# One step of a hybrid diffusion trunk: 32x32 blocks of the triangular inverses turned by TensorE products instead of VectorE transposes

## The chip, the cores and the metric

The kernel runs on one core of a Trainium2 chip. The time is device time of one launch in microseconds. The kernel before took 1106.6 us, the median of three runs (1103.13 to 1106.88). The changed kernel is timed in the same way.

## The reference, cut to what matters

One layer of a trunk works on 640 tokens: 128 context tokens and 512 latent tokens of width 1024. It normalises and modulates x, projects it with one matrix into the inputs of two mixers (a bidirectional RWKV-7 scan with 8 heads of 64, and grouped attention), joins their outputs in one projection, and ends with a gated ConvFFN of inner width 2816.

The change touches the RWKV scan alone. Per head, direction and token the reference does

```python
def step(s, inp):
    r_t, w_t, k_t, v_t, kk_t, a_t = inp
    sa = jnp.einsum('bhvk,bhk->bhv', s, -kk_t)
    s = (s * w_t[:, :, None, :]
         + sa[..., None] * (kk_t * a_t)[:, :, None, :]
         + v_t[..., None] * k_t[:, :, None, :])
    return s, jnp.einsum('bhvk,bhk->bhv', s, r_t)
```

The kernel does 64 tokens at a time. Inside such a chunk each token's correction depends on the earlier ones through a strictly triangular 64x64 matrix L, so that one chunk of one head needs the inverse of (1 - L). These inverses are what `inverse()` makes.

## The kernel before, in words

**Stages.** All of it is one program on five engines. By the profile's time line: the norm and the first projections (0 to about 130 us), the rest of the input projection beside the preparation of the scan (to about 218 us), the inverses, the first steps of the scan and the last projections (to about 310 us), attention beside the scan (to about 600 us), then output projection and FFN (to the end).

**The front.** `s_lora` (line 727) makes decay logits by products into PSUM banks of ring "mi" (two banks), `s_prep` (line 764) turns them on VectorE, ScalarE and GpSimd into AR and BK, and line 819 multiplies these into the matrices L, again into "mi"; line 823 masks them on VectorE into the SBUF tile LT: 128 partitions (two heads of 64 tokens), 32 matrices, 64 columns. Beside it `s_gemm` (line 499) runs the input projection on TensorE.

**The inverses.** There are three units, G0 (heads 0 to 3 of the latent tokens), CX (the context) and G1 (heads 4 to 7), and each calls `inverse` (line 829) once. A unit inverts the 32x32 diagonal blocks of its matrices by forward substitution, with one matrix entry per step for all blocks at once. For that it needs each block laid out along the free dimension of one partition. The kernel before does this with four VectorE transposes of 32x1024 (line 845, into tile Lt), then one addition of Lt and its own transposed view (line 854, into Ls), which folds both scan directions into one triangle. Ls then starts X (twelve small ScalarE copies, lines 858 to 864); 60 small operations follow (lines 870, 871), on VectorE for G0 and CX and on GpSimd for G1 (`EN_INV` is "VG", and G0 is given "V"). Two transposes of X (875, 877) give XT and XN; ScalarE copies their parts into MT (line 890, recorded at the helper's line 377); two sets of TensorE products, W (897, 898) and B (909, 910), fill the off-diagonal blocks, with Ws (901) between them and copies of B into MT behind them.

**Buffers.** G0 and CX share the tags i0 to i3 and the ring "inv" of size one: CX starts only when G0's B has been read out. G1 has tags of its own.

**What follows.** `s_chain` (1033) runs the scan: G0, then CX, then G1, each in two directions; line 1075 multiplies by MT. `s_gemm2` (line 539) makes the projections for g, q and k/v, line 570, in three PSUM banks of ring "tm"; each tile is copied to SBUF (`evac_tm`, line 528) and sent to DRAM (line 464). When gemm2 and G1's inverse are over, their SBUF pools are closed and attention starts by reading these tiles back (`s_norm`, line 1265).

**Order.** Each stage is a generator that yields its next piece of work with an engine and an assumed duration (`T` TensorE, `V` VectorE, `A` ScalarE, `G` GpSimd), or the wait for a ring or an event. `Flow.run` (line 313) keeps a time per engine and picks the piece that can start first, by priority among near ones. Each engine then executes its instructions strictly in the order so made. A wait `ring(name, 2)` is served when two of the ring's places are free.

Of the kernel before, what the change touches and what calls it, by code (L numbers as in the profile page):

```python
# [9 lines left out]
F32 = mybir.dt.float32  # L10
# [3 lines left out]
ALU = mybir.AluOpType  # L14
# [5 lines left out]
P = 128  # L20
# [27 lines left out]
def trunk(ctx: ExitStack, tc: tile.TileContext, a, o, dbg=None):  # L48
    nc = tc.nc
    te, ve, se, ge, sy = nc.tensor, nc.vector, nc.scalar, nc.gpsimd, nc.sync  # L50
# [6 lines left out]
    def nm(s):  # L57
        uid[0] += 1
        return f"{s}_{uid[0]}"
# [31 lines left out]
    mi = lambda s: psr.one("mi", s)  # L91
# [20 lines left out]
    ri = rip.__enter__()  # L112
# [4 lines left out]
    ident = cm2[:, 0:128]  # L117
# [115 lines left out]
    for b in range(4):  # L233
# [3 lines left out]
        g = st.tile([P, 512], F32, name=nm("g"), tag="g", bufs=2)  # L237
# [34 lines left out]
    class Flow:  # L272
# [12 lines left out]
        def ring(f, name, n):  # L285
            f.rings[name] = [f.now] * n
# [71 lines left out]
    def T(us):  # L358
        return ("w", (("T", us),), None, False)

    def V(n, par=False, k=1):
        return ("w", (("V", k * 0.065 + 1.07e-3 * n),), None, par)

    def A(n, tab=None, par=False, k=1):
        return ("w", (("A", k * 0.06 + 0.883e-3 * n),), tab, par)

    def G(us):
        return ("w", (("G", us),), None, False)
# [4 lines left out]
    def VA(n, par=False):  # L373
        return ("w", (("V", 0.065 + 1.07e-3 * n), ("A", 0.06 + 0.883e-3 * n)), None, par)

    def cpy(eng, dst, src):
        (se.copy if eng == "A" else ve.tensor_copy)(dst, src)  # L377
# [4 lines left out]
    def ev_(*key):  # L382
        return ("ev", key)

    flow = Flow()
# [27 lines left out]
    def s_wload(ph, jobs, pl, bufs):  # L413
        for i, dr in enumerate(units_of(jobs)):
            yield ring("raw")
            raw = pl.tile([P, 1024], F32, name=nm("raw"), tag="raw", bufs=bufs)
            sy.dma_start(raw, dr)
            wready["raw", ph, i] = raw
            yield Q(3.5)
            flow.done("raw", ph, i)  # L420
# [227 lines left out]
    G0, G1, CX = Group("g0", (0, 1), 2, 8), Group("g1", (2, 3), 2, 8), Group("ctx", (0, 1, 2, 3), 0, 2)  # L648
# [177 lines left out]
            flow.give(f"ab{d}")  # L826
            flow.done("ab", p, d)

    def inverse(g, en, pl, mp, sfx, rg, bank):
        eng = ve if en == "V" else ge  # L830

        def W(n, k=1):
            return V(n, k=k) if en == "V" else G(0.99 * (k * 0.1 + 2.2e-3 * n))

        nu, LT = g.nu, g.LT
        for p in g.pairs:
            for d in range(2):
                yield ev_("ab", p, d)
        yield ring("inv" + sfx)
        Lt = pl.tile([P, 1024], F32, name=nm("Lt"), tag="i0" + sfx)  # L840
        for qd in range(4):
            pr = slice(32 * qd, 32 * qd + 32)
            t0 = 32 * (qd % 2)
            yield V(1024)
            ve.transpose(Lt[pr].rearrange("p (t s) -> p t s", s=32), LT[pr, :, t0:t0 + 32].rearrange("p u t -> p t u"))
        Ls = pl.tile([P, 32, 32], F32, name=nm("Ls"), tag="i1" + sfx)
        X = pl.tile([P, 1024], F32, name=nm("X"), tag="i2" + sfx)
        X3 = X.rearrange("p (t s) -> p t s", s=32)
        Lt3 = Lt.rearrange("p (t s) -> p t s", s=32)
        yield G(1.0)  # L850
        ge.memset(X, 0.0)
        ge.memset(X[:, ::33], 1.0)
        yield W(1024)
        eng.tensor_tensor(Ls, Lt3, Lt3.rearrange("p t s -> p s t"), ALU.add)

        yield A(496, k=12)
        Lf = Ls.rearrange("p t s -> p (t s)")
        se.copy(X[:, 32::66], Lf[:, 32::66])
        for i in range(2):
            for j in range(2):  # L860
                se.copy(X[:, 64 + 32 * i + j::132], Lf[:, 64 + 32 * i + j::132])
        for b in (4, 8, 16):
            for q in range(0, 32, 2 * b):
                se.copy(X3[:, q + b:q + 2 * b, q:q + b], Ls[:, q + b:q + 2 * b, q:q + b])
        tmp = pl.tile([P, 256], F32, name=nm("tmp"), tag="i3" + sfx)
        for s in range(1, 31):
            n = 31 - s
            yield W(2 * n * s, k=2)
            t3 = tmp[:, :n * s].rearrange("p (t j) -> p t j", j=s)
            eng.tensor_tensor(t3, Ls[:, s + 1:32, s:s + 1].to_broadcast([P, n, s]), X3[:, s:s + 1, 0:s].to_broadcast([P, n, s]), ALU.mult)  # L870
            eng.tensor_tensor(X3[:, s + 1:32, 0:s], X3[:, s + 1:32, 0:s], t3, ALU.add)
        XT = pl.tile([P, 1024], F32, name=nm("XT"), tag="i0" + sfx)
        XN = pl.tile([P, 1024], F32, name=nm("XN"), tag="i1" + sfx)
        yield V(1024)
        ve.transpose(XT, X)
        yield V(1024)
        ve.transpose(XN.rearrange("p (j u) -> p j u", u=32), X3.rearrange("p i j -> p j i"))
        XT3 = XT.rearrange("p (i u) -> p u i", u=32)
        XN3 = XN.rearrange("p (j u) -> p u j", u=32)
        MT = mp[0].tile([P, 2 * nu, 64], F32, name=nm("MT"), tag=mp[1] or "MT" + g.nm)  # L880
        g.MT = MT
        yield G(2.0)
        ge.memset(MT, 0.0)
        fw, bw = slice(0, nu), slice(nu, 2 * nu)
        qs_ = [(slice(64 * e, 64 * e + 32), slice(64 * e + 32, 64 * e + 64)) for e in range(2)]
        for e in range(2):
            q0, q1 = qs_[e]
            for dst, src in ((MT[q0, fw, 0:32], XT3[q0, fw]), (MT[q1, fw, 32:64], XT3[q1, fw]), (MT[q0, bw, 0:32], XN3[q0, bw]), (MT[q1, bw, 32:64], XN3[q1, bw])):
                e2 = yield VA(32 * nu)
                cpy(e2, dst, src)  # L890
        yield ring(rg)
        W3 = bank("W")[:, :32 * nu].rearrange("p (u j) -> p u j", j=32)
        for u in range(nu):
            if u % 4 == 0:
                yield T(0.5)
            for q0, q1 in qs_:
                te.matmul(W3[q1, u], lhsT=LT[q0, u, 32:64], rhs=XN3[q0, u], start=True, stop=True)
                te.matmul(W3[q0, u], lhsT=LT[q1, nu + u, 0:32], rhs=XT3[q1, nu + u], start=True, stop=True)
        yield A(32 * nu)
        Ws = pl.tile([P, 16, 32], F32, name=nm("Ws"), tag="i2" + sfx)  # L900
        se.copy(Ws[:, :nu], W3)
        flow.give(rg)
        yield ring(rg)
        B3 = bank("B")[:, :32 * nu].rearrange("p (u j) -> p u j", j=32)
        for u in range(nu):
            if u % 4 == 0:
                yield T(0.5)
            for q0, q1 in qs_:
                te.matmul(B3[q0, u], lhsT=Ws[q1, u], rhs=XT3[q1, u], start=True, stop=True)
                te.matmul(B3[q1, u], lhsT=Ws[q0, u], rhs=XN3[q0, nu + u], start=True, stop=True)  # L910
        for q0, q1 in qs_:
            e2 = yield VA(32 * nu)
            cpy(e2, MT[q0, fw, 32:64], B3[q0])
            e2 = yield VA(32 * nu, par=True)
            cpy(e2, MT[q1, bw, 0:32], B3[q1])
        flow.give(rg)
        flow.give("inv" + sfx)
        flow.done("inv", g.nm)
# [562 lines left out]
    B_CH, B_FIN, B_INV = 200, 0, 100  # L1481
    B_FR, B_I0 = 0, 0
# [4 lines left out]
    NPB, PR_INV, EN_INV = 6, (0.1, 0.15), "VG"  # L1487
# [8 lines left out]

    fronts = [flow.add(pri, s, {"s_kk": 100, "s_lora": 0, "s_bonus": 0}.get(s.__name__, B_FR)) for pri, s in ((0.9, s_kk()), (1, s_prep(0)), (1.01, s_prep(1)), (PR_LORA, s_lora(0)), (PR_LORA + 0.01, s_lora(1)), (1.1, s_bonus()))]
    weights = [flow.add(3, s_wload(1, jobs1 + jobs2, wpool, 2), 0), flow.add(3, s_wsplit(1, jobs1 + jobs2, wpool, 2), 0)]
    flow.add(1.2, inverse(G0, "V", ri, (ri, None), "", "mi", mi), B_I0)
    flow.run([flow.add(2, s_gemm())])  # L1500

    def evacs():
# [8 lines left out]
    md = lambda s: psc.one("md", s)  # L1511
    cpt = lambda d: psc.p.tile([P, 512], F32, name=nm("cp"), tag=f"cp{d}")
    for d in range(2):
        cpf.append(cpt(d))
        cps.append(cpf[d].rearrange("p (s i v) -> p s i v", s=4, i=2))
    psq = Banks("psq", tm=3)
    flow.ring("tm", 3)
    gemm2 = flow.add(2, s_gemm2(), 100)

# [11 lines left out]
    rp2 = rp2p.__enter__()  # L1531
# [4 lines left out]
    rwkv = []  # L1536
    for d in range(2):
        rwkv += [flow.add(pri, st_(d), {s_chain: B_CH, s_load: 200, s_gram: 100, s_decay: 50}[st_]) for pri, st_ in ((0, s_chain), (0.1, s_load), (0.2, s_gram), (0.2, s_decay))]
    flow.add(PR_INV[0], inverse(CX, EN_INV[0], ri, (rp2, None), "", "md", md), B_INV)
    ipp = pool("ip", side="left")  # L1540
    inv1 = flow.add(PR_INV[1], inverse(G1, EN_INV[1], ipp.__enter__(), (ri, "LTg0"), "x", "md", md), B_INV)
    rwkv += [flow.add(0.5, s_setup(), 100), flow.add(0.75, s_final(), B_FIN)]
    flow.run([gemm2, inv1] + weights)
    evacs()
# [312 lines left out]
    def c_tile(i):  # L1857
        return h2pl.tile([P, 2, 2, H2N - 2], F32, name=nm("c"), tag=f"hr{i % 2}")
# [26 lines left out]
    for i in range(NPL):  # L1885
        c = c_tile(i)
# [79 lines left out]
    for i in range(NPL, 22):  # L1966
# [4 lines left out]
        x = h2pl.tile([P, 3, H2N], F32, name=nm("x"), tag=f"hr{2 + i % 2}")  # L1971
        c = c_tile(i)
# [51 lines left out]
    for tt in range(5):  # L2024
        t = dpl.tile([P, 1024], F32, name=nm("x1t"), tag=f"x1t{tt}", bufs=1)
# [190 lines left out]
```

## Time and profile before

| | us |
|---|---|
| median of three runs | 1106.6 |
| the profiled execution | 1104.36 |
| its span | 1102.6 |
| TensorE busy | 1019.5 (92%) |
| VectorE busy | 790.7 (72%) |
| ScalarE busy | 563.4 (51%) |
| GpSimd busy | 507.4 (46%) |

The span is the time from the first to the last recorded instruction; 1.8 us of the execution lie outside it. Busy shares are means over stages with different limits, so the stages are to be read one by one. A TensorE product of f32 operands stands in the trace as two records.

### The profile page before, as it was taken

To read this page: it belongs to the slowest core of one execution; us is meant where nothing else is said; L and a number is where in the kernel's file an instruction comes from. 1 tells how busy PE (TensorE), PEld (TensorE's weight loads), DVE (VectorE), ACT (ScalarE), POOL (GpSimd) and SP (SyncE) were. 2 spreads that over 40 slices of the span, in tenths; PEclk is the share of its full clock that TensorE was granted. 3 is DMA by queue.
4 is the path that set the end of the run, shared out by engine and by line. 5 is a ranking of instruction groups with operands and counts; after the bars stand their busy time and mean duration, and the time that the engine had idled before them with its cause. 6 is when DMAs were issued, how large, how long until landed. Compare 5 with 4: busy or idle time off the path is not lost. (4 is left out here: it accounts for less than half of the span.)

```text
span 1102.6 us, 20567 instructions
## 1 busy us (share of the span) xinstructions
PE 1019.5 (92%) x8034; PEld 853.6 (77%) x8034; DVE 790.7 (72%) x1367; ACT 563.4 (51%) x1261; POOL 507.4 (46%) x446
## 2 busy tenths in 40 slices
PE   6999998778779999999999988999999998899997
PEld 3788776677665556777777888999999997788885
DVE  3536689989729777465774789999999999643324
ACT  4275433254654767476654764555555556334431
POOL 1234423567415204210202058788888888642330
PEclk8899998889857899799999999999999999899999
DMA  9414534640245684211061421222222223531202
GB/s 364 185 67 116 152 103 133 184 126 21 97 150 194 212 267 136 68 59 61 9 229 74 153 90 44 88 89 94 77 77 78 78 99 112 193 113 58 95 1 96
DMA packets 70433, 127.84 MB, mean 116 GB/s; under 512 B 15664, under 2 KB 41776, under 8 KB 67264
## 3 DMA queue, kind: packets, MB, share of 16 engines
q1 hardware_dynamic: 70336, 126.53, 34.4%
q8 instruction: 63, 1.03, 0.4%
q14 instruction: 34, 0.28, 0.1%
HBM read 105.00 MB, written 21.51 MB: 115 GB/s over the span
## 5 line engine op out<-in xcount | busy, mean ns | idle before, releaser
L1807 POOL TENSOR_TENSOR w<-raw,w 128x512 fp32r<-128x512 f32 (+1 forms) x84 | 153.9, 1839 | 142.6 <-ACT w L1806 121.4
L2050 PE MATMUL dn<-w,ah 128*128 128x512 f32 x660 | 155.7, 398 | 7.9 <-DVE c L1850 7.9
L2050 PEld LDWEIGHTS dn<-w,ah 128*128 128x128 f32 x660 | 125.1, 190 | 38.3 <-issue 8.3
L1844 PE MATMUL up<-tq,w 128*128 128x324 f32 x960 | 150.2, 312 | 2.8 <-DVE x L1989 2.8
L1844 PEld LDWEIGHTS up<-tq,w 128*128 128x128 f32 x960 | 145.2, 190 | 3.1 <-DVE x L1989 3.1
L1844 PE MATMUL up<-hq,w 128*128 128x324 f32 x864 | 137.0, 313 | 4.8 <-ACT w L1806 2.3
L1844 PEld LDWEIGHTS up<-hq,w 128*128 128x128 f32 x864 | 129.6, 188 | 7.8 <-DVE up L1992 4.6
L1807 POOL TENSOR_TENSOR w<-sw,w 128x512 fp32r<-128x512 f32 x80 | 122.4, 1551 | 8.6 <-ACT w L1806 8.6
L1924 DVE TENSOR_TENSOR ah<-act,ah 128x644 fp32r<-128x644 f32 x42 | 58.7, 1415 | 75.8 <-ACT ah L1923 75.8
L1848 ACT ACTIVATE c<-up,pv 128x322 f32<-128x322 f32 x86 | 52.1, 620 | 97.3 <-DVE up L1992 55.6
L432 POOL TENSOR_TENSOR lo<-raw,hi 128x1024 fp32r<-128x1024 f32 x17 | 42.7, 2509 | 68.4 <-ACT hi L430 66.9
L1063 POOL TENSOR_TENSOR SP<-vse,pt 64x128 f32<-64x128 f32 x36 | 14.3, 398 | 128.4 <-DVE vse L1113 127.7
L1923 ACT CAST ah<-act 128x644 fp32r<-128x644 f32 x44 | 31.8, 732 | 76.4 <-PE dn L2050 76.3
L1806 ACT CAST w<-raw 128x512 fp32r<-128x512 f32 (+1 forms) x86 | 63.2, 748 | 5.0 <-PE dn L2050 2.8
L964 PE MATMUL gr<-AK 64*128 64x128 f32 x320 | 47.4, 329 | 11.8 <-ACT DT L377 4.5
L964 PEld LDWEIGHTS gr<-AK 64*128 64x128 f32 x320 | 38.8, 222 | 21.4 <-ACT DT L377 4.7
L1687 PE MATMUL op<-wo,m 128*128 128x512 f32 x192 | 48.3, 404 | 1.7 <-DVE m L1681 1.0
L1849 DVE SCALAR_TENSOR_TENSOR c<-up,pv,c 128x322 f32<-128x322 f32 x86 | 46.5, 543 | 3.8 <-ACT c L1848 3.8
L1806 ACT CAST w<-sw 128x512 fp32r<-128x512 f32 x80 | 47.5, 620 | 2.7 <-PE up L1844 2.7
L1850 DVE SCALAR_TENSOR_TENSOR c<-up,pv,c 128x322 f32<-128x322 f32 x86 | 46.6, 545 | 0.8
L1687 PEld LDWEIGHTS op<-wo,m 128*128 128x128 f32 x192 | 36.7, 194 | 10.5 <-DVE m L1681 1.4
L968 DVE TENSOR_TENSOR GM<-gr,cm 128x512 f32<-128x512 f32 x40 | 26.8, 684 | 21.7 <-PE gr L964 21.3
(335 smaller groups left out, 2485.1 us busy)
## 6 DMA issues: line engine op xcount, KB each, us to landing
wm<-in_wmod SPq DMA_DIRECT2D x24, 1024.0 KB, 6.6
raw<-in_up SPq DMA_DIRECT2D x44, 512.0 KB, 3.3
raw<-in_down SPq DMA_DIRECT2D x22, 512.0 KB, 3.3
AK<-arkd SPq DMA_DIRECT2D x40, 256.0 KB, 4.4
raw<-in_wfm SPq DMA_DIRECT2D x10, 512.0 KB, 5.9
arkd<-AR SPq DMA_DIRECT2D x8, 640.0 KB, 3.7
xT<-in_xT SPq DMA_DIRECT2D x8, 320.0 KB, 6.1
arkd<-BK SPq DMA_DIRECT2D x16, 160.0 KB, 3.5
```

The source lines that it names most:

```text
L432: ge.tensor_tensor(lo, raw, hi.bitcast(F32), ALU.subtract)
L964: te.matmul(ps[par][:, s, i], lhsT=ak[pr, i, 1], rhs=ak[pr, i, 0], start=True, stop=True)
L1687: te.matmul(acc[hf], lhsT=m2[xi][:, k - k0], rhs=wo[k // 2][wi][k % 2][:, 512 * hf:512 * hf + 512], start=(n_mm == 0 and pi == 0), stop=(n ...
L1806: se.copy(hi, raw)
L1807: eng.tensor_tensor(lo, raw, hi.bitcast(F32), ALU.subtract)
L1844: te.matmul(ps, lhsT=wq[wi][:, 128 * k:128 * k + 128], rhs=xq[xi][:, k], start=(first and k == 0 and pi == 0), stop=(last and k == 3 and p ...
L1848: se.activation(c, src[..., 1:H2N - 1], AF.Identity, scale=pv[:, col + 1:col + 2], bias=pv[:, col + 3:col + 4])
L1849: ve.scalar_tensor_tensor(c, src[..., 0:H2N - 2], pv[:, col:col + 1], c, ALU.mult, ALU.add)
L1850: ve.scalar_tensor_tensor(c, src[..., 2:H2N], pv[:, col + 2:col + 3], c, ALU.mult, ALU.add)
L1923: se.copy(t[:, 0, 1:645], act[:, k, 1:645])
L1924: eng.tensor_tensor(t[:, 1, 1:645], act[:, k, 1:645], t[:, 0, 1:645].bitcast(F32), ALU.subtract)
L2050: return [te.matmul(ps, lhsT=(ah, al)[xi][:, p0:p0 + 128], rhs=w2[wi][:, k % 2], start=(k == 0 and pi == 0), stop=(k == 21 and pi == 2)) f ...
```

## The change

Line 840 to 845 go: the tile Lt in SBUF and the four VectorE transposes. In their place 128 TensorE products with 32x32 blocks of the unit matrix write the turned blocks into two PSUM banks, and the one addition of 1024 elements becomes three copies and three additions of 256 elements each on VectorE, from PSUM. The block of the upper triangle is no longer written. For G1 the addition moves from GpSimd to VectorE. The two banks come from ring "mi" for G0 and from ring "tm" for CX and G1; both are returned behind the additions.

```diff
-    def inverse(g, en, pl, mp, sfx, rg, bank):
+    def inverse(g, en, pl, mp, sfx, rg, bank, rl, lbank):
 ...
         yield ring("inv" + sfx)
-        Lt = pl.tile([P, 1024], F32, name=nm("Lt"), tag="i0" + sfx)
-        for qd in range(4):
-            pr = slice(32 * qd, 32 * qd + 32)
-            t0 = 32 * (qd % 2)
-            yield V(1024)
-            ve.transpose(Lt[pr].rearrange("p (t s) -> p t s", s=32), LT[pr, :, t0:t0 + 32].rearrange("p u t -> p t u"))
+
+        yield ring(rl, 2)
+        Lp = [lbank("Lt").rearrange("p (t s) -> p t s", s=32) for _ in range(2)]
+        for t in range(32):
+            if t % 16 == 0:
+                yield T(1.2)
+            for qd in range(4):
+                pr = slice(32 * qd, 32 * qd + 32)
+                te.matmul(Lp[t // 16][pr, t % 16], lhsT=LT[pr, :, 32 * (qd % 2) + t], rhs=ident[pr, pr], start=True, stop=True)
 ...
-        Lt3 = Lt.rearrange("p (t s) -> p t s", s=32)
 ...
-        yield W(1024)
-        eng.tensor_tensor(Ls, Lt3, Lt3.rearrange("p t s -> p s t"), ALU.add)
+
+        yield V(768, k=3)
+        for b in range(2):
+            for c in range(b + 1):
+                ve.tensor_copy(Ls[:, 16 * b:16 * b + 16, 16 * c:16 * c + 16], Lp[b][:, :, 16 * c:16 * c + 16])
+                ve.tensor_tensor(Ls[:, 16 * b:16 * b + 16, 16 * c:16 * c + 16], Ls[:, 16 * b:16 * b + 16, 16 * c:16 * c + 16], Lp[c][:, :, 16 * b:16 * b + 16].rearrange("p t s -> p s t"), ALU.add)
+        for _ in range(2):
+            flow.give(rl)
 ...
-    flow.add(1.2, inverse(G0, "V", ri, (ri, None), "", "mi", mi), B_I0)
+    flow.add(1.2, inverse(G0, "V", ri, (ri, None), "", "mi", mi, "mi", mi), B_I0)
 ...
+    tm = lambda s: psq.one("tm", s)
 ...
-    flow.add(PR_INV[0], inverse(CX, EN_INV[0], ri, (rp2, None), "", "md", md), B_INV)
+    flow.add(PR_INV[0], inverse(CX, EN_INV[0], ri, (rp2, None), "", "md", md, "tm", tm), B_INV)
 ...
-    inv1 = flow.add(PR_INV[1], inverse(G1, EN_INV[1], ipp.__enter__(), (ri, "LTg0"), "x", "md", md), B_INV)
+    inv1 = flow.add(PR_INV[1], inverse(G1, EN_INV[1], ipp.__enter__(), (ri, "LTg0"), "x", "md", md, "tm", tm), B_INV)
```

## Rows read from the trace of the kernel before

**Rows 1.** Table by stretch: us, busy (records) per engine, clock, DMA.
```profile
147.00:218.00 71.00, 59.76 (x501) 47.79 (x496) 69.24 (x103) 21.71 (x47) 28.93 (x18) 0.90 0.51 147
218.00:246.00 28.00, 21.82 (x405) 20.82 (x404) 24.84 (x18) 15.49 (x33) 16.96 (x27) 0.88 0.54 140
246.00:294.00 48.00, 41.77 (x474) 36.67 (x472) 45.28 (x79) 21.07 (x72) 32.60 (x51) 0.96 0.10 34
294.00:345.00 51.00, 41.91 (x556) 31.48 (x556) 24.19 (x48) 30.28 (x72) 10.75 (x20) 0.56 0.48 157
345.00:600.00 255.00, 241.98 (x2476) 175.54 (x2473) 172.00 (x443) 152.50 (x460) 61.95 (x118) 0.93 0.39 133
600.00:940.00 340.00, 323.72 (x2094) 314.29 (x2092) 312.64 (x488) 197.96 (x392) 250.61 (x152) 0.99 0.25 87
```

**Rows 2.** VectorE in order of time: start, us, line, tile [idle before].
```profile
147.17 0.69 DVE L823 SCALAR_TENSOR_TENSOR LT<-lt,cm 128x512 f32<-128x512 f32 x1 [3.13 <-PE lt L819]
147.90 8.04 DVE L845 STREAM_TRANSPOSE Lt<-LT 32x1024 f32<-32x1024 f32 x4
...
157.37 1.98 DVE L854 TENSOR_TENSOR Ls<-Lt 128x1024 f32<-128x1024 f32 x1
...
218.37 1.25 DVE L875 STREAM_TRANSPOSE XT<-X 128x1024 f32<-128x1024 f32 x1
219.54 2.04 DVE L877 STREAM_TRANSPOSE XN<-X 128x1024 f32<-128x1024 f32 x1
221.51 7.79 DVE L845 STREAM_TRANSPOSE Lt<-LT 32x1024 f32<-32x1024 f32 x4
...
235.40 8.08 DVE L845 STREAM_TRANSPOSE Lt<-LT 32x1024 f32<-32x1024 f32 x4
243.51 1.39 DVE L377 COPY MT<-B 32x512 f32<-32x512 f32 x2
...
245.54 0.41 DVE L377 COPY e<-tm 128x256 f32<-128x256 f32 x1
245.87 2.34 DVE L854 TENSOR_TENSOR Ls<-Lt 128x1024 f32<-128x1024 f32 x1
```

**Rows 3.** VectorE, one step of the substitution, 240 elements from SBUF.
```profile
190.55 0.40 DVE L870 TENSOR_TENSOR tmp<-Ls,X 128x240 f32<-128x240 f32 x1
```

**Rows 4.** TensorE in order of time: G0's W products, first and last of 128 records.
```profile
222.50 0.22 PE L897 MATMUL W<-XN,LT 32*32 32x32 f32 x1
...
224.27 0.23 PE L898 MATMUL W<-XT,LT 32*32 32x32 f32 x1
```

**Rows 5.** TensorE in order of time: the end of the front.
```profile
204.39 1.38 PE L819 MATMUL lt<-AR,BK 64*64 64x64 f32 x40 [0.42 <-ACT v L377]
...
212.48 2.40 PE L819 MATMUL lt<-AR,BK 64*64 64x64 f32 x40 [6.71 <-DVE LT L823]
```

**Rows 6.** GpSimd in order of time: G1's addition, first and last substitution steps.
```profile
229.39 2.87 POOL L854 TENSOR_TENSOR Ls<-Lt 128x1024 f32<-128x1024 f32 x1 [2.99 <-DVE Lt L845]
...
234.45 0.32 POOL L870 TENSOR_TENSOR tmp<-Ls,X 128x30 f32<-128x30 f32 x1
...
292.13 0.25 POOL L871 TENSOR_TENSOR X<-X,tmp 128x30 f32<-128x30 f32 x1
```

**Rows 7.** ScalarE in order of time: G0's last copy, then G1's eight and gemm2's last.
```profile
244.93 0.58 ACT L377 COPY MT<-B 32x512 f32<-32x512 f32 x1 [10.51 <-DVE MT L377]
...
298.81 2.19 ACT L377 COPY MT<-XT 32x512 f32<-32x512 f32 x2
...
303.60 4.23 ACT L377 COPY MT<-XN 32x512 f32<-32x512 f32 x4
...
309.00 0.37 ACT L377 COPY e<-tm 128x256 f32<-128x256 f32 x1
```

**Rows 8.** SyncE's queue in order of time: attention's first load.
```profile
309.85 3.18 SPq L1265 DMA_DIRECT2D qk<-qkd  x5
```

**Rows 9.** TensorE in order of time: gemm2's last product.
```profile
302.06 0.28 PE L570 MATMUL tm<-lo,hhi 128*128 128x256 f32 x1
```

## The prediction

> **What bounds the kernel now.** I read the table by stretch first, then VectorE in order of time, then the neighbours of what ends there. From 345 us on TensorE is busy for 242 of 255 us and then for 324 of 340 us [rows 1]: that part is TensorE's own work, the change leaves it alone, and it starts as much earlier as what lies before it ends earlier. So the question is when attention starts. In the stretch 147 to 218 us VectorE is busy for 69.2 of 71.0 us while TensorE has 11.2 us free: there VectorE sets the pace. From 218 to 294 us VectorE is still the fullest engine (70.1 of 76 us), with TensorE at 63.6 us. From 294 to 345 us nobody is full and TensorE's granted clock is 0.56, near the lower of its two levels (1.2 of 2.4 GHz): a stretch of waits [rows 1].
>
> That stretch begins with the start of attention. Its first load is issued at 309.85 us [rows 8], right behind ScalarE's copy of gemm2's last tile at 309.00 us; that copy stands in ScalarE's order behind the eight copies of G1's MT, which end at 307.8 us [rows 7], and those wait for G1's substitution on GpSimd, which ends at 292.4 us [rows 6]. The product that filled the tile was over at 302.3 us [rows 9]. So two things gate attention, a few us apart: G1's inverse, through ScalarE's order, and TensorE's last gemm2 product.
>
> **The change part by part.** *VectorE loses per unit* four transposes: 8.04, 7.79 and 8.08 us for the three units [rows 2]. G0 and CX also lose the addition, 1.98 and 2.34 us on VectorE [rows 2]; G1 loses 2.87 us on GpSimd [rows 6].
>
> *VectorE gains per unit* three copies and three additions of 256 elements from PSUM. A copy of just this size out of PSUM took 0.41 us [rows 2], so 1.23 us for three. For an addition that reads PSUM with a stride no row exists. From below: 240 elements from SBUF took 0.40 us [rows 3], so 0.41. From above: the two transposes of X differ in that the second reads with a stride, 2.04 against 1.25 us [rows 2], a factor of 1.6, so 0.41 x 1.6 = 0.66. Three additions are 1.2 to 2.0 us; I take the middle, 1.65, since L854 itself mixes a plain and a strided operand. Per unit 2.9 us (2.4 to 3.2). The net on VectorE is then 10.0 - 2.9 = 7.1 us for G0, 10.4 - 2.9 = 7.5 us for CX, and 7.8 - 2.9 = 4.9 us for G1.
>
> *TensorE gains per unit* 128 products of 32x32 by 32x32. G0's W products have the same shape and sit on four tiles of the array as the new ones do; 64 of them (128 records) took from 222.50 to about 224.3 us, 1.8 us [rows 4]. So 128 cost 3.6 us per unit, 10.8 us in all. The new products load weights with a stride of 64 elements, which the W products do not; with the factor of 1.6 from above it would be 5.8 us per unit. I take 3.6, from the row of the same shape, and keep 5.8 for the range. The planner counts 2.4 us for them, so it will think TensorE freer than it is.
>
> *The front, 147 to 218 us.* The last L products of the front stand in TensorE's queue from 204.4 us and are held until 212.48 us, 6.71 us of it a visible wait for VectorE [rows 5]. VectorE would be there 7.1 us earlier, at 205.4 us. TensorE, with 3.6 us more to do behind 147.9 us, reaches them at 204.4 + 3.6 = 208.0 us. The later of the two counts: 208.0 instead of 212.5, a gain of 4.5 us. It would be 7.1 if TensorE found the 3.6 us elsewhere, and nothing if the two "mi" banks are held so long that the front's own products, which use the same two, starve VectorE. Against that stands G0's own substitution: it gives VectorE ready work at any time until 218 us, so I cost the hold at nothing; without that cover it would cost what the banks are held, 3.6 + 2.9 = 6.5 us.
>
> *From 218 us.* G1 went from the start of its transposes at 221.51 us to its first substitution step at 234.45 us in 12.9 us: transposes, addition on GpSimd, ScalarE's small copies [rows 2, 6]. Now its products can run under the transposes of X (218.4 to 221.5 us [rows 2]), and the path is 2.9 us on VectorE and the remaining 2.2 us (12.9 - 7.8 - 2.9): 5.1 us, a gain of 7.8 us. For CX the tag i0 no longer binds the transposed blocks, but Ls and X take tags that G0's B products read, so it still waits for G0 to end; its own gain is the net 7.5 us, and 4.9 us of G1's lie ahead of it. G0's MT, whose last ScalarE copy waited 10.51 us for VectorE behind the transposes of both other units [rows 7], is complete that much earlier, so the scan starts earlier. By VectorE and GpSimd alone attention would move by 7.8 us.
>
> TensorE doesn't let it. From 218 us to its last gemm2 product at 302.3 us it has about 84 us, of which 12.4 us are free until 294 us [rows 1] and perhaps 3.5 us behind that: 68 us of work. Two units bring 7.2 us more: 75 us. In the shorter stretch of 84 - 7.8 = 76.5 us it would have to be 98% busy, in an order in which every product waits for other engines. In the front, where it has the work, it reaches 84% [rows 1]. I let it reach 92%, as over the whole kernel: 75 / 0.92 = 81.8 us, which is 2.5 us less than 84.3. So 2.5 us of the 7.8 come through; what is late next is gemm2's last product instead of G1's copies.
>
> The wait for two banks of "tm" is new. Queued behind it on TensorE are gemm2's tiles, which then have one bank of three; I cost it inside the 92% and give the bad case as a rival. No DMA is added, removed or moved past SyncE's queue by these lines; attention's loads there [rows 8] move with what releases them.
>
> The sum against the profiled execution: 1104.4 - 4.5 - 2.5 = 1097.4 us. That execution lies 2.2 us under the median of 1106.6 and inside the runs (1103.1 to 1106.9), so a median may lie one or two us above the sum. I say 1098.
>
> **A rule against it.** For blocks of 32x32 inside a group of partitions, the Trainium skill ("VectorE: DVE Perf Modes", section on rules for kernel authors) holds VectorE's transpose to be the fastest way. In the rows a unit's transposes and addition cost 10.0 us on one engine, and the new way 3.6 + 2.9 = 6.5 us on two, so the rule isn't borne out for these strided reads; what it would give is the second rival's time. The skill's page "TensorEngine Tiling (Array Packing)", section "PSUM Bottleneck", says that packing small products speeds up TensorE and leaves the copy out of PSUM as the limit. Here 2.9 us of copying stand beside 3.6 us of products; if the rule held, the first rival's time would follow.
>
> **The rivals.** *1. VectorE stays the limit and TensorE's products find free time.* Then the gains are 7.1 and 7.8 us: 1104.4 - 14.9 = 1089.5 us. For it: 27 us of TensorE's time are free between 147 and 302 us, and less waiting would hold its clock up, which was 0.90 and 0.88 [rows 1]. Against it: the free time lies in waits and not where the products are due.
>
> *2. Nothing is won, because TensorE takes it all.* If the products cost 5.8 us per unit, the front gains 212.5 - 210.2 = 2.3 us, and the later stretch needs (68 + 11.6) / 0.92 = 86.5 us, 2.2 us more than now: 1104.4 us. For it: TensorE is the fullest engine of the kernel, and the strided load has no row. Against it: the free time above.
>
> *3. Slower: CX's two "tm" banks are held over G0's end.* The place is TensorE's queue at about 222 us. If CX's products are ordered ahead of G0's B products, their banks can't be emptied until B has been read, since Ls and X take buffers of G0; until then gemm2 turns in one bank, and each tile waits for its copy. The last tile took 7.1 us from its product to the end of its copy (302.3 to 309.4 us [rows 7, 9]). Two tiles so delayed cost 14 us, of which the front's 4.5 are returned: 1104 - 4.5 + 14 = 1114 us. It decides from the point at which gemm2's last product falls behind 309 us. For it: the planner knows rings, and it undercounts the products. Against it: CX's ring wait stands behind "inv", which G0 gives only at its end.
>
> **How the numbers follow.** Forecast 0.52, with its own range of 1092 to 1102; the first rival 0.13, the second 0.20, the third 0.15. The range is 1087 to 1112: below it some two us under the first rival; above it the second rival whole, and most of the third is left out. A difference of under 0.5% (5.5 us) can't be told from no change. Faster than 1101.1 us are the first rival and most of the forecast: 0.59. Within 0.5% are the second and a rest of the forecast: 0.25. Slower: 0.16.
>
> **What would show it.** No record of a VectorE transpose at the place of L845; VectorE's six operations at 0.4 to 0.7 us each; 256 TensorE records per unit in about 3.6 us; the wait before the front's last L products down from 6.7 to under 3 us; the first substitution step on GpSimd near 222 us instead of 234.45; attention's first load near 303 instead of 309.85 us; the rest unchanged in length. I am wrong if that load moves by less than 2 us or later, if VectorE's additions take over 1 us, or if the stretch of attention behind 345 us changes its length by more than the start moved.

## The result, and the profile after

The changed kernel takes 1130.8 us, the median of four runs (1129.44 to 1131.97), against 1106.4 us before: a ratio of 1.0227, 95% interval 1.0204 to 1.0249. It is slower, where 1098 us and a gain had been forecast. The profiled span is 1128.5 us (before 1102.6).

The table by stretch of the changed kernel, columns as in [rows 1]:

```profile
147.00:218.00 71.00, 61.34 (x770) 49.11 (x768) 54.22 (x81) 21.75 (x46) 30.14 (x17) 0.91 0.47 134
218.00:246.00 28.00, 14.87 (x579) 13.84 (x579) 14.61 (x37) 13.72 (x30) 4.90 (x9) 0.57 0.62 156
246.00:294.00 48.00, 41.77 (x682) 36.48 (x682) 40.01 (x91) 17.33 (x67) 24.30 (x43) 0.85 0.16 54
294.00:345.00 51.00, 47.76 (x695) 41.89 (x695) 11.89 (x23) 27.55 (x71) 22.25 (x41) 0.87 0.20 66
345.00:600.00 255.00, 220.78 (x2362) 156.15 (x2362) 176.34 (x440) 146.06 (x435) 67.17 (x122) 0.94 0.40 133
600.00:940.00 340.00, 331.35 (x2090) 317.66 (x2089) 301.37 (x487) 191.81 (x389) 237.46 (x152) 0.99 0.27 92
```

Against [rows 1] VectorE is relieved where it was full: 54.2 instead of 69.2 us in the first stretch, 14.6 instead of 24.8 in the second. Nothing comes of it. TensorE falls from 21.8 to 14.9 us in the second stretch, which holds 579 records against 405 because CX's 128 new products, 256 records, lie in it, and from 242.0 to 220.8 us in the stretch of attention. Over 147 to 600 us TensorE is idle for 66.5 us instead of 45.8: 20.7 of the 25.9 us of span are lost there as idle time. It is lost behind 345 us. Up to there TensorE is as busy as before (165.7 of 198 us against 165.3), but 13.1 us of it are the new products, so that less of the old work is done by then.

The start of gemm2 in the kernel before, on TensorE:

```profile
214.81 0.63 PE L556 MATMUL fm<-hhi,hi 128*128 128x320 f32 x1
```

TensorE in order of time, changed kernel: start, us, tile, records, idle time before:

```profile
174.39 2.02 PE L848 MATMUL Lt<-cm,LT 32*32 32x32 f32 x128
...
213.98 2.40 PE L819 MATMUL lt<-AR,BK 64*64 64x64 f32 x40 [5.05 <-DVE LT L823]
...
220.48 2.73 PE L848 MATMUL Lt<-cm,LT 32*32 32x32 f32 x176
...
229.15 0.23 PE L905 MATMUL W<-XN,LT 32*32 32x32 f32 x1 [5.94 <-DVE XN L885]
...
236.91 0.45 PE L848 MATMUL Lt<-cm,LT 32*32 32x32 f32 x16 [5.32 <-issue]
...
238.98 0.26 PE L917 MATMUL B<-XT,Ws 32*32 32x32 f32 x1 [1.62 <-ACT Ws L909]
...
241.32 0.63 PE L556 MATMUL fm<-hhi,hi 128*128 128x320 f32 x1
...
247.09 2.70 PE L848 MATMUL Lt<-cm,LT 32*32 32x32 f32 x176
...
257.28 0.60 PE L556 MATMUL fm<-hhi,hi 128*128 128x320 f32 x1 [2.31 <-DVE Ls L860]
...
353.36 0.36 PE L570 MATMUL tm<-lo,hhi 128*128 128x256 f32 x1
```

Three things stand here. G0's products begin at 174.39 us, 25 us after the last L matrix they read is masked. Most of CX's products (176 of 256 records at 220.48) stand ahead of G0's W and B and of gemm2; TensorE then waits for VectorE, on "issue" (no wait that the profile shows) and for ScalarE. gemm2's first product comes at 241.32 us, where in the kernel before it came at 214.81 us, and its second tile waits at 257.28 us for the additions that empty G1's banks. gemm2's last product starts at 353.36 us instead of 302.06 [rows 9].

VectorE of the changed kernel in order of time:

```profile
148.62 0.69 DVE L823 SCALAR_TENSOR_TENSOR LT<-lt,cm 128x512 f32<-128x512 f32 x1 [3.13 <-PE lt L819]
...
180.40 0.39 DVE L859 COPY Ls<-Lt 128x256 f32<-128x256 f32 x1
180.83 0.42 DVE L860 TENSOR_TENSOR Ls<-Ls,Lt 128x256 f32<-128x256 f32 x1
...
225.97 1.25 DVE L883 STREAM_TRANSPOSE XT<-X 128x1024 f32<-128x1024 f32 x1
...
241.23 0.42 DVE L859 COPY Ls<-Lt 128x256 f32<-128x256 f32 x1 [12.22 <-PE B L918]
```

GpSimd of the changed kernel, G1's first substitution step:

```profile
257.79 0.25 POOL L878 TENSOR_TENSOR tmp<-Ls,X 128x30 f32<-128x30 f32 x1 [13.76 <-ACT X L866]
```

SyncE's queue of the changed kernel, attention's first load:

```profile
363.19 1.00 SPq L1273 DMA_DIRECT2D qk<-qkd  x2
```

The new operations on VectorE cost no more than was forecast, 0.39 to 0.42 us each. But XT of G0 comes at 225.97 us instead of 218.37 [rows 2], CX's first copy waits 12.22 us for B, G1's first substitution step comes at 257.79 instead of 234.45 us [rows 6], and attention's first load at 363.19 instead of 309.85 us [rows 8].

### The profile page after: what moved, and what is told of

Its sections match the earlier page's. It is cut to its first block, busy times and chain, and to the rows that moved or that the text cites. A ratio compares the mean times of both kernels' runs of the same rounds, so it can differ in the third digit from the quotient of the medians.

```text
span 1128.5 us, 22163 instructions
## 1 busy us (share of the span) xinstructions
PE 1024.8 (91%) x8802; PEld 859.9 (76%) x8802; DVE 765.4 (68%) x1378; ACT 558.0 (49%) x1246; POOL 511.1 (45%) x453
## 3 DMA queue, kind: packets, MB, share of 16 engines
q1 hardware_dynamic: 70336, 126.53, 33.6%
## 5 line engine op out<-in xcount | busy, mean ns | idle before, releaser
L1853 PEld LDWEIGHTS up<-hq,w 128*128 128x128 f32 x864 | 132.5, 192 | 5.9 <-DVE up L2001 3.1
L972 PE MATMUL gr<-AK 64*128 64x128 f32 x320 | 41.1, 311 | 2.4 <-DVE gT L377 2.4
L1863 DVE TENSOR_TENSOR act<-c 128x644 f32<-128x644 f32 x22 | 38.5, 1750 | 4.6 <-ACT c L1862 4.5
L972 PEld LDWEIGHTS gr<-AK 64*128 64x128 f32 x320 | 33.5, 206 | 10.0 <-issue 2.8
```

The costliest lines, as they stand in the source:

```text
L972: te.matmul(ps[par][:, s, i], lhsT=ak[pr, i, 1], rhs=ak[pr, i, 0], start=True, stop=True)
L1853: te.matmul(ps, lhsT=wq[wi][:, 128 * k:128 * k + 128], rhs=xq[xi][:, k], start=(first and k == 0 and pi == 0), stop=(last and k == 3 and p ...
L1863: ve.tensor_tensor(act[:, i, 1:645], c[:, 0].rearrange("p n t -> p (n t)"), c[:, 1].rearrange("p n t -> p (n t)"), ALU.mult)
```

## The experiments

T1 says that the loss comes from G0's wait for both "mi" banks in the front; T2, from CX and G1 holding two of gemm2's three "tm" banks; T3, from the products' own time on TensorE. T4 to T6 are said where they come up. Each edit can also change the order that the planner writes, and which engine gets a small copy, so a run shows the edit together with its order. This table has what all runs showed; starts in us, ratio to the kernel before with its interval:

| run | gemm2 first | gemm2 last | attention's first load | ratio |
|---|---|---|---|---|
| before | 214.8 | 302.1 | 309.9 | 1 |
| changed | 241.3 | 353.4 | 363.2 | 1.0227 [1.0204, 1.0249] |
| e1_g0_old | 238.5 | 367.4 | 376.3 | 1.0446 [1.0407, 1.0485] |
| e2_g0_only | 222.2 | 301.9 | 303.1 | 1.0033 [1.0008, 1.0058] |
| e3_wait_mi | 227.8 | 338.0 | 342.9 | 1.0162 [1.0119, 1.0205] |
| e4_one_bank | 220.5 | 343.5 | 353.7 | 1.0186 [1.0124, 1.0248] |
| e5b_mi_g0old | 219.1 | 311.3 | 313.7 | 1.0018 [0.9989, 1.0047] |
| e5_all_mi | 221.7 | 312.2 | 314.6 | 0.9990 [0.9971, 1.0010] |
| e3b_wait_tm | 217.1 | 288.4 | 292.8 | 1.0032 [1.0000, 1.0065] |
| n2_cost1900 | 225.8 | 379.2 | 388.4 | 1.0477 [1.0440, 1.0514] |
| e10_twice | 227.6 | 344.2 | 345.8 | 1.0289 [1.0253, 1.0325] |
| e5c_mi_one | 219.9 | 319.8 | 321.0 | 1.0149 [1.0111, 1.0187] |
| e4b_one_bank_g0 | 222.4 | 295.9 | 298.0 | 0.9997 [0.9963, 1.0032] |
| e9_fm_first | 219.8 | 350.8 | 352.7 | 1.0226 [1.0183, 1.0269] |
| e11_boost400 | 224.4 | 354.0 | 365.4 | 1.0330 [1.0291, 1.0369] |
| e14_mi_g0first | 197.9 | 271.0 | 273.1 | 1.0202 [1.0153, 1.0251] |

### Which unit: G0 the old way, or G0 alone the new way

In these, `None` means the four transposes and the addition of the kernel before.

```diff
-inverse(G0, "V", ri, (ri, None), "", "mi", mi, "mi", mi)
+inverse(G0, "V", ri, (ri, None), "", "mi", mi, None, None)
```

> G0 goes back to VectorE's transposes; CX and G1 keep the products in two 'tm' banks. T1 (the loss comes from G0's wait for both 'mi' banks in the front): the front is that of before, XT of G0 near 218 us instead of 226, and the time falls to 1100 to 1108 us. T2 (the loss comes from CX holding two of three 'tm' banks over G0's end): G0 ends on time, but gemm2's first fm product still waits for B, near 233 us (241 less the 8 us of the front) against 214.8 before; the time stays at 1117 to 1125 us. T3 (TensorE pays for the products themselves, 3.6 us per unit, at 91% busy): a third of the loss goes, about 1122 us, but gemm2 begins as early as before.

```diff
-inverse(CX, ..., "md", md, "tm", tm)
-inverse(G1, ..., "md", md, "tm", tm)
+inverse(CX, ..., "md", md, None, None)
+inverse(G1, ..., "md", md, None, None)
```

> Only G0 by products in two 'mi' banks; CX and G1 by VectorE's transposes as before. T1: the front stays as in the changed kernel, G0's products begin near 174 us though LT is there at 149, XT near 226 us; the time is 1114 us (7.6 us later) or more. T2: the front loses its 7.6 us or less and gemm2's first fm product comes before G0's W products as in the kernel before, near 222 us; the time is 1106 to 1114 us. T3: a third of the loss, about 1114 us, with the loss as busy time of TensorE (3.6 us) and not as idle gaps.

Measured 1154.3 and 1108.2 us. T1 falls: without G0's new way the loss is all there, and larger, above what any of the three expected. With it alone 0.3% is left, although XT of G0 then comes at 238.2 us, 20 us late. The e1 run loses more than the changed kernel: from 400 to 500 us TensorE was as busy (89.5 and 90.7 us) but ran 783 records against 1027, at a granted clock of 0.67 against 0.92. Why the clock fell there isn't settled.

### The wait without the products, and the products without the double wait

```diff
+        if g is G0:
+            yield ring("mi", 2)
         Lt = pl.tile([P, 1024], F32, name=nm("Lt"), tag="i0" + sfx)
...
         eng.tensor_tensor(Ls, Lt3, Lt3.rearrange("p t s -> p s t"), ALU.add)
+        if g is G0:
+            for _ in range(2):
+                flow.give("mi")
```

> The kernel before, with one thing added: G0's inverse waits in the planner for two places of 'mi' and holds them until its addition is issued; it puts nothing into them, and VectorE transposes as before. T1: the wait alone delays G0: its first transpose comes near 174 us instead of 147.9, XT near 226 to 234 us, the time 1112 to 1122 us. T2 and T3: no products and no 'tm' place taken, so 1104 to 1109 us.

```diff
-        yield ring(rl, 2)
+        for b in range(2):
+            yield ring(rl)
+            Lp = lbank("Lt").rearrange("p (t s) -> p t s", s=32)
...
+            flow.give(rl)
```

> All three units by products, but one bank at a time: 64 products into one bank, three VectorE operations that empty it, the place given back, then the second half. The work is the same, 128 products and six VectorE operations per unit; only the two places held at once are gone. T1 and T2 together (the waits for two places are the loss): G0 begins near 150 us, gemm2's tiles keep two of the three 'tm' places, and the time is 1095 to 1108 us. T3: the products are all there, so 1125 to 1131 us. If CX's single place is still held over G0's end, gemm2's first fm product comes no later than some 10 us after before's, and the time is 1106 to 1115 us.

Measured 1119.5 and 1124.6 us: by the time alone e3 seems to speak for T1, and what T2 and T3 expected (1104 to 1109 us) is missed, but T1's place is wrong. The first transpose came at 150.3 us, not 174. What moved is gemm2: its first product stood behind G0's W, at 227.8 us. In e4 the time is nearest to the 1125 us of T3 and outside what the others expected. There 15 of gemm2's 48 first products ran from 220.5 us, the next at 254.25 us. These 15 are part of a tile of 24 that had its bank, so it was the order on TensorE that held the first tile back, not the lack of a bank.

### Only the ring: "mi" for CX and G1

```diff
-inverse(CX, ..., "md", md, "tm", tm)
-inverse(G1, ..., "md", md, "tm", tm)
+inverse(CX, ..., "md", md, "mi", mi)
+inverse(G1, ..., "md", md, "mi", mi)
```

> All three units by products as in the changed kernel, but CX and G1 in the 'mi' banks. T2: gemm2 stands ahead of G0's W again, its first fm product near 222 us as with G0 alone (1108 us), and the time is 1098 to 1112 us. T3 (the products' own time on TensorE) and T4: 1125 us or more.

The same with G0 the old way:

> G0 by VectorE's transposes; CX and G1 by products, two banks at once, but in the two 'mi' banks instead of two of gemm2's three 'tm' banks. Against the run with G0 old and 'tm' banks (1154 us) only the ring differs. T2 as it now stands (CX's products stand ahead of gemm2 and hold its banks until G0 has ended): gemm2's 48 fm products begin near 215 us, ahead of G0's W as in the kernel before, its last product ends near 305 to 315 us, and the time is 1098 to 1112 us. T4 (it is the products of CX and G1 themselves, wherever their banks are): 1135 us or more.

Measured 1101.7 and 1105.8 us. The same products, two banks at once as before, other banks: the whole loss is gone, of the changed kernel (1.0227 to 0.9990) as of e1 (1.0446 to 1.0018). So the loss comes with taking the banks from "tm", as T2 says; T4, and T3 as the cause of the 2.3%, fall. Whether the banks held on the chip do it or the order written because of them, these two runs can't tell. TensorE of e5_all_mi, in order of time:

```profile
221.66 0.64 PE L556 MATMUL fm<-hhi,hi 128*128 128x320 f32 x1
...
230.47 0.21 PE L905 MATMUL W<-XN,LT 32*32 32x32 f32 x1 [0.40 <-DVE XN L885]
...
241.86 0.26 PE L917 MATMUL B<-XT,Ws 32*32 32x32 f32 x1
...
312.16 0.28 PE L570 MATMUL tm<-lo,hhi 128*128 128x256 f32 x1
```

gemm2 stands ahead of W and between W and B, so that G0's serial path runs under it; W waits 0.40 us there, against 5.94 in the changed kernel.

### The plan alone: places without products, and a cost without a change

```diff
+        if g is not G0:
+            yield ring("tm", 2)
         Lt = pl.tile([P, 1024], F32, name=nm("Lt"), tag="i0" + sfx)
...
+        if g is not G0:
+            for _ in range(2):
+                flow.give("tm")
```

> The kernel before, in which CX and G1 wait in the planner for two places of 'tm' and give them back after their addition, with VectorE's transposes as before: no product and no bank is held on the chip. If the wait for places in the plan alone displaced gemm2, the time would be 1120 us or more and gemm2's first fm product near 238 us. If the banks held on the chip by the products do it (T2), gemm2 starts at 215 us and the time is 1102 to 1112 us.

```diff
-            yield V(1024)
+            yield V(1900)
             ve.transpose(Lt[pr].rearrange("p (t s) -> p t s", s=32), LT[pr, :, t0:t0 + 32].rearrange("p u t -> p t u"))
```

> The kernel before with one figure of the planner changed: it counts each VectorE transpose of the inverses as 1900 elements (2.1 us) instead of 1024 (1.2 us). No instruction is added or removed; only the order written for each engine can change. T5 (the time hangs on where gemm2 stands against G0's W and B in TensorE's queue, whatever moved it): W then stands ahead of gemm2's first fm product, the last product of gemm2 ends some 30 us later than in the kernel before, and the time is 1112 to 1122 us. If order matters little, 1103 to 1108 us.

Measured 1105.8 and 1156.1 us. Waiting for the places in the plan, without products in them, does no harm. And n2, which only changes what the planner believes, loses 4.8%, over twice what was expected of it: the order alone can cost more than the change. (A few small operations also go to another engine: VectorE runs 1363 instead of 1367, GpSimd 453 instead of 446.) Its TensorE, in order of time:

```profile
223.90 0.26 PE L897 MATMUL W<-XN,LT 32*32 32x32 f32 x1
...
225.84 0.63 PE L556 MATMUL fm<-hhi,hi 128*128 128x320 f32 x1
...
238.94 0.26 PE L909 MATMUL B<-XT,Ws 32*32 32x32 f32 x1 [8.87 <-ACT Ws L901]
...
379.15 0.28 PE L570 MATMUL tm<-lo,hhi 128*128 128x256 f32 x1
```

W first, then 21 products of gemm2, then 8.87 us of waiting for Ws. The e3 run has the same order up to B, yet its gemm2 ends 41 us earlier. The difference lies late: from 315 to 370 us n2's TensorE starts 20 of the 240 "tm" products, with the scan and G1's W and B between them. Why the planner's order puts them so is open.

### The place in the queue, or the banks

```diff
         yield ring("inv" + sfx)
+        if g is not G0:
+            yield ev_("u", 1)
         yield ring(rl, 2)
```

> The changed kernel with one wait added in the planner: CX and G1 ask for their two 'tm' banks only when gemm2's fm tiles are finished. The products, the banks and the two places held stay. T2: the 48 fm products stand ahead of G0's B again (near 222 to 235 us instead of 241 to 263), so part of the loss goes; but CX's products then hold two of three banks while gemm2's 240 tm products wait, so gemm2 ends later than 320 us, and the time is 1108 to 1125 us. If only the start of gemm2 counts: 1100 to 1108 us.

```diff
-    gemm2 = flow.add(2, s_gemm2(), 100)
+    gemm2 = flow.add(2, s_gemm2(), 400)
```

> The changed kernel with one figure altered: gemm2's boost is 400 instead of 100, so that its first fm tile stands ahead of G0's W in TensorE's queue; CX and G1 hold two 'tm' banks as before, and gemm2 has one. If the place in the queue is the loss: gemm2's last product near 310 us instead of 353, time 1100 to 1110 us. If the lack of banks is the loss: the first fm tile comes near 222 us, but the second only when CX's bank is given back near 245 us, gemm2 ends behind 335 us, and the time is 1115 to 1132 us.

Measured 1128.2 and 1138.8 us, so an early start of gemm2 isn't enough. In e11, with its first tile ahead of W (224.39 us), its second starts at 252.03 us and its last product at 354 us, as in the changed kernel. In e9 all 48 first products come early, the next at 269.17 us; TensorE of e9 behind that:

```profile
272.71 0.29 PE L570 MATMUL tm<-lo,hhi 128*128 128x256 f32 x1
...
301.80 0.58 PE L570 MATMUL tm<-hi,hhi 128*128 128x256 f32 x1
...
308.43 0.38 PE L570 MATMUL tm<-hi,hhi 128*128 128x256 f32 x1 [2.07 <-DVE Ls L862]
```

Both times lie above what was expected, by 3 and 7 us. The rows show two things at work. gemm2 does wait for banks that the inverses hold: for 2.31 us in the changed kernel (257.28 us), 2.07 us in e9 (308.43 us) and 1.96 us in e11 (265.37 us), each time until an addition on VectorE has emptied one. But it is also put behind other work without such a wait. In e9 it stops after 12 of a tile's 24 products, from 273 to 301.8 us, and in the changed kernel after 19, from 246 to 252.0 us, though these tiles have their bank; in e11 the second tile follows G1's products at once, 11 us after ScalarE has read the first. And e3, e5c (below) and n2 lose 1.5 to 4.8% though gemm2 keeps its three banks on the chip. So two pairs of runs put the loss on the ring (e5_all_mi against the changed kernel, e5b against e1); how much of it is the hold on the chip and how much the order written around it is not separated.

### The price of a product

```diff
-                te.matmul(Lp[t // 16][pr, t % 16], ...)
+                for _ in range(2):
+                    te.matmul(Lp[t // 16][pr, t % 16], ...)
```

> All three units by products with CX and G1 in the 'mi' banks (1101.7 us), and each product issued twice into the same place, so that TensorE does 10.8 us of products more, in nearly the same order. T3 (TensorE pays for the products): 1107 to 1112 us. If the stretch before 345 us, where TensorE was busy 169.6 of 198 us in that run, hides them: 1099 to 1105 us.

Measured 1135.2 us, 33.6 us more than e5_all_mi and three times what T3 asked for. TensorE of e10_twice in order of time:

```profile
182.92 2.08 PE L849 MATMUL Lt<-cm,LT 32*32 32x32 f32 x128 [2.47 <-issue]
...
252.99 2.07 PE L849 MATMUL Lt<-cm,LT 32*32 32x32 f32 x127 [1.94 <-issue]
256.37 2.08 PE L849 MATMUL Lt<-cm,LT 32*32 32x32 f32 x128 [1.31 <-issue]
```

The DMA queues of e10_twice from 246 to 284 us: packets, MB, share of 16 engines:

```profile
q1 hardware_dynamic: 432, 0.79, 5.7%
q8 instruction: 10, 0.16, 1.8%
```

After a run of some 128 records TensorE mostly stands for 1.3 to 2.5 us on "issue", waiting for nothing that the profile shows: 15.1 us in ten such gaps from 147 to 345 us, against 2.2 us in e5_all_mi and 6.8 us in the changed kernel. Over these 198 us TensorE does some 12.6 us of products more than in e5_all_mi, and yet it is busy for 164.8 us against 169.6. So it does about 17 us less of the other work: 12.6 us go to the products and 4.8 us are more idle time. Of the 32 us by which gemm2 ends later the rest isn't explained; the order differs too (its first product comes at 227.6 instead of 221.7 us). So a product of this size is not free; in e5_all_mi the idle time of TensorE held it, in e10 it didn't.

### Can the gain be had?

The one-bank form as in e4, for G0 alone; then for all three units, from "mi"; last, e5_all_mi with G0 put ahead of the front's streams:

> Only G0 by products, one 'mi' bank at a time; CX and G1 by VectorE's transposes. Beside the run with G0 in two banks (1108 us) it shows what the hold of two places costs in the front. T1: its products begin near 150 us instead of 176, and the time is some 6 us less, 1098 to 1104 us. T2 and T6: G0's start is worth nothing while gemm2 stands ahead of W; the products may begin early or late, and the time stays at 1102 to 1110 us.

> All three units by products, all in the 'mi' banks, one bank at a time: no place of gemm2 is taken and no two places are held at once. T2: as with both 'mi' banks, 1098 to 1106 us. T6 (behind 345 us TensorE is the limit, and it gains nothing from an earlier attention load or a freer VectorE, so no order of this change gains more than 0.5%): not under 1097 us. If the banks held in the front still cost the 4.5 us that the prediction counted as a gain, about 1095 us.

```diff
-    flow.add(1.2, inverse(G0, "V", ri, (ri, None), "", "mi", mi, "mi", mi), B_I0)
+    flow.add(0.85, inverse(G0, "V", ri, (ri, None), "", "mi", mi, "mi", mi), B_I0)
```

> All three units by products with CX and G1 in the 'mi' banks, and G0's inverse given priority over the front's other work (0.85 instead of 1.2), so that its products come near 150 us and its substitution ends some 20 us earlier than 227 us. The front's gain of 4.5 us, if it can be had: 1094 to 1100 us. T6 (nothing ahead of gemm2's end is worth anything unless gemm2 itself ends earlier, and even then nothing below an attention load of some 310 us): 1098 to 1108 us. If the front's own L products come late for it: 1110 us or more.

Measured 1101.4, 1119.6 and 1124.8 us. None beats the kernel before beyond the interval. In e4b G0's products begin at 175.1 us even with one bank asked for, and in e14 at 173.0 us even at the higher priority. So neither the second bank nor the priority decides when they start; and in e3, with the wait for both places, the first transpose came at 150.3 us. The table by stretch, 149 to 174 us, of the changed kernel:

```profile
149.00:174.00 25.00, 25.00 (x144) 17.80 (x143) 14.02 (x15) 8.53 (x14) 7.21 (x6) 1.00 0.41 125
```

The same stretch of the kernel before:

```profile
149.00:174.00 25.00, 22.08 (x126) 16.16 (x125) 24.20 (x37) 9.45 (x25) 5.78 (x4) 0.90 0.34 113
```

TensorE is busy for all of these 25 us with the front's own work, at a granted clock of 1.00: as far as these rows show, the products stand in a full queue, while VectorE, which had turned the blocks at once, falls from 24.2 to 14.0 us. In e14 gemm2 ends 31 us early and attention's load comes at 273 us, but the front's last L products are pushed to 252 to 258 us (before 204 to 215 [rows 5]), and with them CX, G1 and the scan: the first uvo copy of the scan comes at 297.3 instead of 261.9 us. In e5c, where T2 and T6 expected no more than 1106 us, gemm2 ends 8 us later than in e5_all_mi and 1.5% are lost though no inverse takes a "tm" bank; why is open.

## Why the prediction was wrong, step by step

**The prices were nearly right.** The copies and additions took 0.39 to 0.42 us where 0.41 and 0.55 were forecast; the strided reading of PSUM costs hardly more than a copy. The products took 2.02 us per 128 records at best and 4.4 us per unit on average (13.1 us for three), against 3.6 forecast. The forecast's own row gave more: it took 1.8 us from the first W product to the start of the last, and that last one ends at 224.50 us, 2.0 us behind the first start [rows 4]. What had no term is the "issue" time, 6.8 us in all. The longest gap, 5.32 us between G0's W and B, held nothing up by itself: behind it B waited 1.62 us more for Ws, which ScalarE made right behind its copies of MT, at 238.34 us.

**The front failed in its first line.** "TensorE, with 3.6 us more to do behind 147.9 us" took it for granted that the products run where the transposes ran. They ran 25 us later, with TensorE busy throughout, and the substitution with them. The wait before the last L products went from 6.71 to 5.05 us instead of under 3, and G0's XT came 7.6 us later instead of 4.5 us earlier. This cost little in the end (e2, e4b); that gemm2 filled TensorE meanwhile is the likely reason.

**The wait for "tm" was costed at nothing.** "I cost it inside the 92% and give the bad case as a rival" is the step that made the sign wrong: e5_all_mi differs from the changed kernel in the ring alone, and in the order that follows from it, and is 2.4% faster, some 26 us. The term put at nothing is worth that much. Rival 3 had the place, and part of the mechanism: CX's banks are emptied only behind G0's B (VectorE's wait of 12.22 us). But gemm2 did not turn in one bank meanwhile; it did not start at all until 241.32 us. So its size was off: it counted two tiles of 7.1 us, while gemm2 started 26.5 us and ended 51.3 us late. It was held unlikely because CX's ring wait stands behind "inv", which G0 gives only at its end. In the plan that is so; in TensorE's queue CX's products stand ahead of G0's W all the same, as the rows show. The code suggests why: the order on the chip also follows each stream's boost, 100 for CX and 0 for G0. For CX and G0 that was not tried alone; e11, where gemm2's boost is the only edit and its first tile comes at 224.39 instead of 241.32 us, agrees with it.

**The premise was wrong too.** The prediction let everything behind attention's start move with it. The table of runs refutes this. With the load at 293, 298, 303, 310, 314 or 315 us (e3b, e4b, e2, before, e5b, e5) the ratios lie between 0.999 and 1.003: a load that is 17 us earlier gains nothing. TensorE is busy for 240 to 242 of the 255 us behind 345 us in e3b, e4b, before and e5; the row of e3b_wait_tm:

```profile
345.00:600.00 255.00, 241.44 (x2511) 175.07 (x2511) 161.35 (x426) 152.75 (x459) 57.49 (x113) 0.95 0.40 138
```

It seems that the scan fills TensorE there when attention isn't ready, and attention when the scan waits. All nine kernels with the load at 321 us or later lose 1.5 to 4.8%: attention is then left alone at the end. In the changed kernel the scan's last uvo copy came at 536.2 us and attention's last product at 608.7 us; before, at 551.1 and 580.6 us. An early load is no help by itself: e14, with the load at 273 us, loses 2.0%, with a scan that starts late (297.3 us). So even with the banks put right, the forecast gain of 7.0 us found nothing to come from: the change relieves VectorE and adds to TensorE, which had 13 of 255 us free behind 345 us.

**The first rival's condition** (products find free time) was met in e5_all_mi, and its 1089.5 us did not come, for the same reason. The second rival's time, 1104.4 us, is the one that e5_all_mi comes near, though not for the reason given: the products cost 4.3 us per unit there, not 5.8.

## What to carry to other kernels

An operation moved to another engine joins that engine's queue: before pricing it, look at where in the new queue it will stand, and what is busy there at that moment. Ask of a borrowed buffer ring what gates its release, not only how long the borrower works: here CX's banks could be emptied only behind G0's B, and borrowing this ring instead of the other cost 2.4%. And where a planner writes the order, run a null change (here one cost figure) to see how far the planner's choices alone move the time.

## What the runs showed of the hardware

In e10_twice dense small products outrun their instructions. 128 records with their 128 weight loads are 256 instructions and take 2.07 us; then TensorE mostly stands for 1.3 to 2.5 us, and the instruction queue brought 10 packets with 0.16 MB in the 38 us shown, 16 KB each. The packets' times in the trace tie the two together: each of the ten gaps of e10_twice and the three of the changed kernel ended 1.25 to 1.51 us after such a packet had landed. In the changed kernel one gap was 5.32 us, from 231.59 us; its packet started only at 234.12 us. The DMA engines were 62% busy in that stretch, but that they delayed the packet is not shown. The Trainium skill ("Runtime: NRT & Kernel Launch", section "Instruction fetch mechanics") says that instructions come in blocks of 16 KiB, 256 of them, and that the fetch is hidden behind the issue of instructions. The block size agrees with these rows; the hiding doesn't, for products of 16 ns per record.
